# A layer with two FFNs and a mixer: the order of the next FFN's row sums against a norm's root

## The chip, the cores and the metric

The kernel runs on one core of a Trainium2 chip. The core has a matrix engine (TensorE, PE in the profile), a vector engine (VectorE, DVE), a scalar engine (ScalarE, ACT), GpSimd (POOL) and SyncE (SP), which here issues the transfers between device memory and the core's memories. Each engine works off its own list of instructions in a fixed order, and waits by semaphores for what other engines deliver. The metric is the device time of one execution in microseconds, the median over some runs.

## The reference

One layer on a sequence of 1024 tokens with width 1024, in three parts, each added to the stream `x`: a first FFN (SwiGLU, inner width 2816), a mixer, and a second FFN. Each part starts with a norm that is modulated by numbers from a condition vector:

```
mod = silu(cond) @ w_mod + b_mod;  sh1, sc1, g1, ..., sh3, sc3, g3 = split(mod, 9)
h  = modulate(rms_norm(x, mix_norm), sh2, sc2);  b, c, v, u = split(h @ w_in)
yA = b * conv3(c * v);  yB = GLU(ssm(u))
x  = x + g2 * ([rms_norm(yA) | rms_norm(yB)] @ w_out)
h  = modulate(rms_norm(x, ffn2_norm), sh3, sc3)
x  = x + 0.5 * g3 * (silu(h @ w_gate) * (h @ w_up)) @ w_down
```

Shift, scale and gate (`sh3`, `sc3`, `g3`) of the second FFN depend on the condition alone. They are 3 x 1024 dot products of length 1024.

## The kernel before

Activations lie with the width on the 128 partitions and tokens along the free axis, in two halves `h` of 512 tokens; a width of 1024 makes 8 tiles `d` or `k`. Every operand of a product is split into a high part (rounded to fp32r) and a low part, and a product is three matrix products (`mm3`, from line 337). Weights stream through two raw buffers (loaded on SP), and `Weights.pump` splits each: ACT casts the high part, DVE subtracts to get the low part. Split weights go to a ring of four tiles in this stage; a tile comes free when its last product is done.

In the mixer, PE does in this order: products for `u`, `c`, `v` with the state-space work between, the `b` products, the GLU products (`gl`, in `glu`), and the output products (`wo`, in `w_out`). Two norms are needed ahead of `wo`: that of the conv part (`nA`, halves `nAa`, `nAb`) and that of the SSM part (`nBa`, `nBb`). A norm goes like this: squares on ACT, added up on DVE; PE sums over partitions (tile `...st`); `roots` runs nine small DVE instructions on 128 x 4 numbers; `wide` widens the result to 128 x 512 (`...rb`), and adds that instruction to the list `widened`; PE spreads it over the partitions (`...bc`, in `spread`); DVE scales (`oat`, `obt`) and ACT and DVE split (`oa`, `ob`). The norm of the second FFN follows in the same way, as `n3a` and `n3b`; there some of the sums of squares are added on POOL.

The dot products for the second FFN's modulation are made on DVE beside all this. `mod_fetch` loads a tile of 128 x 1024 of transposed `w_mod` into one of two buffers `wm`; `mod_vector` multiplies it by the broadcast condition and sums each row into one column of `scl`, `mods` or `gate`. There are 24 of these reductions (in the profile `wm<-wm,cact`, each with a read of the accumulator): 8 for the scale, then 8 for the shift, then 8 for the gate. Each is followed by the fetch for the one two places later.

When each of them is emitted is set by a `Clock` that ticks with every `mm3`. Work that is due after so many ticks is emitted then (`clock.after`), and every `clock.period` ticks one step of a side generator is taken; `side2` gives one reduction per step. In the mixer the period is 8 during the second half of the `b` products, 1000 (none) during `glu` and the first `w_out` calls, and 3 from the call `w_out((2, 3), 1, 0)` on; what is left is emitted behind `w_out((4, 5, 6, 7), 0, 1)`.

The order of emission is not that of execution. From this point of the program on (`InOrder.strict` is false) the framework's planner fixes each engine's order before the run: in a simulated time of its own cost model, an engine takes the first instruction in program order among those whose inputs and buffers it believes ready. An instruction emitted late can so be placed early on its engine, into a gap that the planner sees. `InOrder.follow` adds an edge without a semaphore between two instructions of one engine: the first argument may not be placed ahead of the second.

Of the kernel before, what the change touches and what calls it, by code (L numbers as in the profile page):

```python
# [17 lines left out]
ALU = mybir.AluOpType  # L18
# [217 lines left out]
def hymba_layer(ctx: ExitStack, tc, x_d, xt_d, wm1_d, wmod_d, gu1_d, gs1_d, ds1_d, wl1_d, win_d, wout_d, glu_d, gu2_d, gs2_d, wd2_d, ds2_d, wl2_d, cols_d, cond_d, lam_d, bc_d, out_d):  # L236
    nc = tc.nc
    V, A, T, SP = (InOrder(tc, e) for e in (nc.vector, nc.scalar, nc.tensor, nc.sync))
# [15 lines left out]
    pools = {}  # L254
# [158 lines left out]
    widened = []  # L413
# [52 lines left out]

    def mod_vector(w, s):

        V.tensor_tensor_reduce(out=w, in0=w, in1=pools["cact"][:], scale=1.0, scalar=0.0, op0=ALU.mult, op1=ALU.add, accum_out=s)

    later = [(n, b, i) for n in (G1, SC2, SH2, G2, SC3, SH3, G3) for b in range(4) for i in range(2)]
    fetched = deque()
# [8 lines left out]
    def mod_tile(home):  # L481

        n, d, r = fetched.popleft()
        dst = (mods, scl, gate)[n % 3][:, n // 3]
        mod_vector(r, dst[:, d : d + 1])
        if d == KT - 1:
            mod_done(n, 0, KT, dst)
        mod_fetch(home)
# [308 lines left out]
    cact = pools["cact"] = cap.tile([P, 1024], F32, name="cact")  # L797
# [815 lines left out]
        gate_b(i, 0)  # L1613
    clock.until(lambda: NB - 1 not in held)
    sp_open.close()
    yp2 = es2.enter_context(tc.tile_pool(name="yp2", bufs=1))
    yb = [yp2.tile([P, S], F32, tag=f"yb{i}", name=f"yb{i}") for i in range(4)]
    mods_open = ExitStack()
# [74 lines left out]
        clock.step()  # L1693
    clock.period = 4
    mods_open.close()
    es2.close()
    movs["B"] = ctx.enter_context(tc.tile_pool(name="movB", bufs=12))
    norm_into(act3, 0, n3[0], 2, "h3", "B", copied3)
# [180 lines left out]
```

## Time and profile before

| what | us |
|---|---|
| median of 3 runs | 1709.91 |
| runs | 1709.65, 1709.91, 1714.65 |
| profiled execution, its time | 1713.61 |
| span in its trace, first to last instruction | 1711.8 |
| PE busy | 1668.0 (97%) |
| DVE busy | 1250.9 (73%) |
| ACT busy | 624.3 (36%) |
| POOL busy | 402.7 (24%) |

A row of a timeline gives the start from the beginning of the span, the length (of all that are merged in it), the engine, the line of the kernel, the operation, the tiles written and read, the shapes and the number of instructions; in brackets stands how long the engine was idle before it, and what ended that. Line 112 is the helper through which every call goes, so groups are told apart by the tiles' names. A row of stretches gives for each engine its busy time and, in brackets, its instructions, then the granted clock of PE, the share of the transfers and their rate.

### The profile page before, as it was taken

To read this page: it belongs to the slowest core of one execution; us is meant where nothing else is said; L and a number is where in the kernel's file an instruction comes from. 1 tells how busy PE (TensorE), PEld (TensorE's weight loads), DVE (VectorE), ACT (ScalarE), POOL (GpSimd) and SP (SyncE) were. 2 spreads that over 40 slices of the span, in tenths; PEclk is the share of its full clock that TensorE was granted. 3 is DMA by queue.
4 is the path that set the end of the run, shared out by engine and by line. 5 is a ranking of instruction groups with operands and counts; after the bars stand their busy time and mean duration, and the time that the engine had idled before them with its cause. 6 is when DMAs were issued, how large, how long until landed. Compare 5 with 4: busy or idle time off the path is not lost.

```text
span 1711.8 us, 20820 instructions
## 1 busy us (share of the span) xinstructions
PE 1668.0 (97%) x7532; PEld 1369.1 (80%) x7532; DVE 1250.9 (73%) x1957; ACT 624.3 (36%) x1056; POOL 402.7 (24%) x309
## 2 busy tenths in 40 slices
PE   7999999999999999999999999999999999999997
PEld 4888787888878778787877778888888888888886
DVE  7739698899588997635657877957777767576645
ACT  5425333333354332332214325524444434322233
POOL 6012333323222322100000021122233223333212
PEclk8999999999999999999999999999999999999998
DMA  8312464454565656134644352324443343759212
GB/s 340 131 47 97 142 220 163 148 161 159 205 221 171 230 196 233 50 100 145 221 145 153 130 184 103 119 74 172 185 185 148 148 172 148 267 227 382 107 50 99
DMA packets 101625, 281.48 MB, mean 164 GB/s; under 512 B 19345, under 2 KB 34961, under 8 KB 90386
## 3 DMA queue, kind: packets, MB, share of 16 engines
q1 hardware_dynamic: 101522, 280.15, 46.5%
q8 instruction: 59, 0.97, 0.2%
q14 instruction: 44, 0.36, 0.1%
HBM read 195.69 MB, written 76.02 MB: 159 GB/s over the span
## 4 chain that ended last, share of the span: by engine, by line
PE 50%; DVE 4%; DMA 3%; issue 0%; ACT 0%; SPq 0%; DVEq 0%; ACTq 0%
PE wo L112 4%; PE fb10d L112 2%; PE u L112 2%; PE fbd_1B L112 2%; PE fbd_0B L112 2%; DMA swz<-si 2%; PE b L112 2%; PE c L112 1%; PE fb0u L112 1%; PE fbd_1C L112 1%; PE fbd_0C L112 1%; PE fbd_1A L112 1%; PE fbd_0A L112 1%; PE fb0d L112 1%; PE fb0g L112 1%; PE v L112 1%
## 5 line engine op out<-in xcount | busy, mean ns | idle before, releaser
L112 ACT CAST w<-raw 128x512 fp32r<-128x512 f32 (+1 forms) x374 | 240.3, 677 | 483.7 <-issue 77.1
L112 DVE TENSOR_TENSOR w<-raw,w 128x512 fp32r<-128x512 f32 (+1 forms) x374 | 307.0, 840 | 117.9 <-ACT w L112 117.0
L177 POOL TENSOR_TENSOR raw<-sums,raw 128x512 f32<-128x512 f32 x54 | 81.9, 1517 | 441.8 <-DVE w L112 429.5
L168 POOL TENSOR_TENSOR sums<-raw 128x512 f32<-128x512 f32 x54 | 75.4, 1396 | 266.7 <-DMA raw<-in_ds 136.4
L179 POOL TENSOR_TENSOR raw<-raw 128x512 f32<-128x512 f32 x54 | 83.3, 1543 | 82.0 <-DVE w L112 82.0
L112 DVE CUSTOM_DVE_ANT_0 wm<-wm,cact 128x1024 f32<-128x1024 f32 x56 | 78.0, 1406 | 11.0 <-DMA wm<-in_wmod 10.7
L169 POOL TENSOR_TENSOR raw<-raw 128x512 f32<-128x512 f32 x54 | 84.5, 1565 | 4.2
L370 POOL TENSOR_TENSOR n3aq<-n3aq,n3aq 128x512 f32<-128x512 f32 x5 | 7.7, 1532 | 275.5 <-ACT n3aq L112 275.3
L112 DVE TENSOR_TENSOR w<-sums,w 128x512 fp32r<-128x512 f32 x54 | 54.1, 1013 | 2.7 <-ACT w L112 2.2
L112 PE MATMUL p<-h,w 128*128 128x512 f32 x192 | 51.5, 420 | 1.7 <-ACT h L112 1.7
L112 PE MATMUL wo<-oa,w 128*128 128x512 f32 x192 | 46.1, 393 | 1.2 <-DVE w L112 0.7
L112 PE MATMUL v<-h,w 128*128 128x512 f32 x192 | 46.9, 395 | 0.0
L112 PE MATMUL c<-h,w 128*128 128x512 f32 x192 | 46.6, 394 | 0.0
L112 PE MATMUL b<-h,w 128*128 128x512 f32 x192 | 45.6, 393 | 0.0
L112 PE MATMUL wo<-ob,w 128*128 128x512 f32 x192 | 45.5, 392 | 0.1
L112 PEld LDWEIGHTS p<-h,w 128*128 128x128 f32 x192 | 37.1, 200 | 10.1 <-ACT h L112 1.9
L112 PE MATMUL u<-h,w 128*128 128x512 f32 x192 | 44.8, 392 | 0.2 <-DVE h L112 0.2
L112 ACT CAST w<-sums 128x512 fp32r<-128x512 f32 x54 | 32.8, 620 | 31.8 <-PE fa4gE L112 2.2
L112 PEld LDWEIGHTS wo<-oa,w 128*128 128x128 f32 x192 | 35.7, 188 | 9.7 <-DVE w L112 1.1
L112 PEld LDWEIGHTS u<-h,w 128*128 128x128 f32 x192 | 35.7, 188 | 8.3 <-DVE h L112 0.6
L112 PEld LDWEIGHTS wo<-ob,w 128*128 128x128 f32 x192 | 35.7, 188 | 7.8 <-ACT ob L112 0.5
L112 PEld LDWEIGHTS b<-h,w 128*128 128x128 f32 x192 | 35.5, 188 | 7.2
(1579 smaller groups left out, 4054.0 us busy)
## 6 DMA issues: line engine op xcount, KB each, us to landing
raw<-in_gs SPq DMA_DIRECT2D x38, 1024.0 KB, 4.9
wm<-in_wmod SPq DMA_DIRECT2D x56, 512.0 KB, 4.8
raw<-in_ds SPq DMA_DIRECT2D x16, 1024.0 KB, 6.6
mw<-in_wm SPq DMA_DIRECT2D x8, 1024.0 KB, 7.6
raw<-in_win SPq DMA_DIRECT2D x8, 1024.0 KB, 5.9
raw<-in_gu SPq DMA_DIRECT2D x6, 1024.0 KB, 5.3
raw<-in_wl SPq DMA_DIRECT2D x5, 1024.0 KB, 6.7
xb<-in_xt SPq DMA_DIRECT2D x8, 512.0 KB, 6.8
```

Source lines behind the costliest of these rows:

```text
L112: r = getattr(self.engine, name)(*args, **kw)
L168: self.G.tensor_tensor(out=f, in0=r[2], in1=r[1], op=ALU.subtract)
L169: self.G.tensor_tensor(out=r[1], in0=r[1], in1=r[0], op=ALU.subtract)
L177: self.G.tensor_tensor(out=r, in0=s["t3"], in1=r, op=ALU.add)
L179: self.G.tensor_tensor(out=r, in0=self.chunk(j, 3), in1=r, op=ALU.subtract)
L370: nc.gpsimd.tensor_tensor(out=a, in0=a, in1=sq[:, :n], op=ALU.add)
```

## The change

While the mixer runs (a mark `mixed` in `pools`, set where the SSM buffers are closed and taken away when the mixer's buffers are), every reduction of `mod_vector` gets an edge to the last element of `widened`, that is, to the last root that had been widened by then in program order. The planner may not place the reduction ahead of it on DVE.

```
     def mod_vector(w, s):
 
-        V.tensor_tensor_reduce(out=w, in0=w, in1=pools["cact"][:], scale=1.0, scalar=0.0, op0=ALU.mult, op1=ALU.add, accum_out=s)
+        r = V.tensor_tensor_reduce(out=w, in0=w, in1=pools["cact"][:], scale=1.0, scalar=0.0, op0=ALU.mult, op1=ALU.add, accum_out=s)
+        if "mixed" in pools:
+            V.follow(r, widened[-1])
...
     sp_open.close()
+    pools["mixed"] = True
...
     mods_open.close()
+    pools.pop("mixed")
     es2.close()
```

## The prediction

> **What bounds the kernel now.** The reductions are numbered R1 to R24 in program order: R1 to R8 make `scl`, R9 to R16 `mods`, R17 to R24 `gate` of the second FFN. I read the page first, for the engine with the work.
>
> ```profile
> PE 1668.0 (97%) x7532; PEld 1369.1 (80%) x7532; DVE 1250.9 (73%) x1957; ACT 624.3 (36%) x1056; POOL 402.7 (24%) x309
> ```
>
> PE is busy for 97%, so only time in which PE stands still, or runs at a lower clock, can be gained. Next, what PE waited for (us in total, times, longest); the rows of the mixer behind its gate products are these:
>
> ```profile
> PE nBabc L112 <- DVE nBarb L112: 2.3, 1, 2.3
> PE nAbbc L112 <- DVE nAbrb L112: 1.7, 1, 1.7
> PE gl L112 <- DVE yg L112: 1.7, 1, 1.7
> PE nBbbc L112 <- DVE nBbrb L112: 0.7, 1, 0.7
> PE wo L112 <- DVE w L112: 0.7, 1, 0.7
> ```
>
> Two of them, the first and the last but one, wait for a widened root of the SSM norm (`nBa`, `nBb`). The timeline of DVE shows what stood in front of these roots (start, length):
>
> ```profile
> 948.39 0.16 DVE L112 TENSOR_SCALAR nBanv<-nBast 128x4 f32<-128x4 f32 x1 [0.25 <-PE nBast L112]
> 949.06 0.16 DVE L112 TENSOR_SCALAR nBani<-nBanv 128x4 int32<-128x4 int32 x1
> 949.13 1.22 DVE L112 CUSTOM_DVE_ANT_0 wm<-wm,cact 128x1024 f32<-128x1024 f32 x1
> ...
> 951.44 1.23 DVE L112 TENSOR_TENSOR w<-raw,w 128x1024 fp32r<-128x1024 f32 x1 [1.01 <-ACT w L112]
> 952.58 0.15 DVE L112 TENSOR_TENSOR nBana<-nBana,nBanv 128x4 f32<-128x4 f32 x1
> 952.65 1.22 DVE L112 CUSTOM_DVE_ANT_0 wm<-wm,cact 128x1024 f32<-128x1024 f32 x1
> 953.80 0.16 DVE L112 SCALAR_TENSOR_TENSOR nBany<-nBana,nBani 128x4 f32<-128x4 f32 x1
> ...
> 954.78 0.43 DVE L112 TENSOR_SCALAR nBarb<-nBany 128x512 f32<-128x512 f32 x1
> 955.12 1.22 DVE L112 CUSTOM_DVE_ANT_0 wm<-wm,cact 128x1024 f32<-128x1024 f32 x1
> ...
> 970.19 1.22 DVE L112 CUSTOM_DVE_ANT_0 wm<-wm,cact 128x1024 f32<-128x1024 f32 x1
> 973.79 1.22 DVE L112 CUSTOM_DVE_ANT_0 wm<-wm,cact 128x1024 f32<-128x1024 f32 x1
> 977.00 0.43 DVE L112 TENSOR_SCALAR nBbrb<-nBbny 128x512 f32<-128x512 f32 x1
> ```
>
> These `wm` rows are reductions: R5 and R6 (949.13, 952.65) sit inside the chain of small root instructions of `nBa`, R7 and R8 behind it (R7 is shown), R9 and R10 (970.19, 973.79) ahead of the widened root of `nBb`. Between them `w`, the low part of a weight tile, waits 1.01 us for ACT. PE and its clock just behind (two rows of its timeline, the chain's row for twelve `gl` products and one for full speed, and between them two stretches, whose third figure from the end is the granted clock):
>
> ```profile
> 955.35 1.36 PE L112 MATMUL nBabc<-ident,nBarb 128*128 128x128 f32 x8 [2.30 <-DVE nBarb L112]
> 937.29 1.16 PE L112 MATMUL nAbbc<-ident,nAbrb 128*128 128x128 f32 x8 [1.75 <-DVE nAbrb L112]
> 956.71 4.13 PE gl L112 x12
> 956.00:958.00 2.00, 2.00 (x9) 1.71 (x8) 1.94 (x5) 1.01 (x2) 0.00 (x0) 0.53 0.56 162
> 958.00:960.00 2.00, 2.00 (x7) 1.52 (x7) 2.00 (x4) 0.22 (x1) 0.00 (x0) 0.62 0.77 233
> 1049.62 5.44 PE fb0g L112 x24
> ```
>
> After the wait the granted clock falls to 0.53 and 0.62. The twelve `gl` products take 4.13 us; 24 products at full clock take 5.44, so twelve take 2.72. The fall costs about 1.4 us on `gl` and, by the 1.36 of `nBabc` against the 1.16 us of the same eight products of `nAbbc`, 0.2 more: **1.6 us**.
>
> **The change part by part.** Counted along the program's ticks: R1 is emitted before any root of the mixer, R2 to R4 after `nAa` was widened, and R5 to R24 from the first tick of the second `w_out` pair on, after `nBb`. So R1 to R4 keep their place (the 1.7 us waits at `gl` and `nAbbc` stay), and R5 to R10 can't start until `nBbrb` has been issued. No instruction is added or removed; six of 1.22 us, their accumulator reads, and the DMA issues on SP that refill their two buffers, are moved.
>
> *The nBa wait.* Without R5 and R6 the chain is `nBani` at 949.06, then seven steps at 0.2 us each (from 953.80 to 954.78 there are five, in 0.98 us), and `nBarb` with 0.43: it starts near 950.6 and is done near 951.1. PE finishes its `gl` products at 953.05 (955.35 less 2.30). The low part of the weights is the doubt. If it stays behind the first step, it still ends near 952.58, for it waits for ACT, and only R6 goes: the step that started at 953.80 starts 0.2 us after 952.58, 1.02 us sooner, and so does `nBarb`. If it comes behind the root, the whole 2.30 goes. The planner took it only after 1.2 us of R5, and the chain to the root lasts 1.5 us, so it lands near its end; each step behind it then costs 0.2. I take **1.8 us**, between 1.02 and 2.30.
>
> *The clock.* A wait of 0.5 us in place of 2.30 should not lower it: the wait of 1.7 us at `gl` left it at 1.00, as a stretch of 10 us shows (same columns),
>
> ```profile
> 920.00:930.00 10.00, 7.98 (x39) 6.11 (x38) 7.14 (x18) 5.21 (x9) 0.00 (x0) 1.00 0.00 2
> ```
>
> so 1.6 us would go, from the profiled execution. The Trainium skill, "TensorE: Matmul & The Clock Gate", Part 1, has the clock halve after an idle window of about 3.4 us that runs freely, at another phase in every run; by its length alone the wait of 2.30 us would not do it, and the trace has it fall. By its free phase a fall need not come in each execution; then the 1.6 us is not in all of them.
>
> *The nBb wait.* R9 and R10 leave that chain, 2.4 us of work; `nBbrb`, now at 977.00, is then ready before PE comes, even when updates of `x` stay among its steps. The whole **0.7 us**; nothing at the least, if a weight tile takes their place.
>
> *What is late next.* The reductions end in the same DVE queue, later. Behind `nBbrb` both buffers are full, so R5 and R6 run at once; the others are paced by their transfers:
>
> ```profile
> 978.91 1.23 DVE L112 CUSTOM_DVE_ANT_0 wm<-wm,cact 128x1024 f32<-128x1024 f32 x1 [1.49 <-DMA wm<-in_wmod]
> 990.64 1.72 POOL L370 TENSOR_TENSOR n3bq<-n3bq,n3bq 128x512 f32<-128x512 f32 x1 [14.49 <-ACT n3bq L112]
> 991.13 2.31 DVE L112 CUSTOM_DVE_ANT_0 wm<-wm,cact 128x1024 f32<-128x1024 f32 x1
> 1014.15 1.23 DVE L112 CUSTOM_DVE_ANT_0 wm<-wm,cact 128x1024 f32<-128x1024 f32 x1 [3.47 <-DMA wm<-in_wmod]
> 1024.21 1.23 DVE L112 CUSTOM_DVE_ANT_0 wm<-wm,cact 128x1024 f32<-128x1024 f32 x1 [1.21 <-DMA wm<-in_wmod]
> 1025.36 2.72 DVE L112 SCALAR_TENSOR_TENSOR x<-wo,gate,x 128x512 f32<-128x512 f32 x4
> 1034.03 0.43 DVE L112 TENSOR_SCALAR n3arb<-n3any 128x512 f32<-128x512 f32 x1
> 1014.95 11.04 PE L112 MATMUL wo<-ob,w 128*128 128x512 f32 x48
> 1031.27 0.95 PE L112 MATMUL n3ast<-one,n3aq 128*128 128x1 f32 x8
> 1036.99 1.05 PE L112 MATMUL n3abc<-ident,n3arb 128*128 128x128 f32 x8
> 1097.72 21.76 PE fb0d L112 x96
> ```
>
> From R20 (1014.15) to R24 (1024.21) a reduction takes 2.5 us. At 978.91 R11 ran in the profile; after the change that place is R7's, so the tail lags by four, 10 us at most: R24 at 1034 in place of 1024. Its results are not the limit: `gate` is read behind the first down products, on PE from 1097.72, and with a lag of four R16, the last for `mods`, runs where R20 does now, at 1014.15, while its reader needs `n3abc` at 1036.99. SP issues the refills in one queue with the raw weights; a refill now waits until after `nBbrb`, and a raw load put behind it by the planner would wait too. No row of PE's waits in the mixer names a transfer, so I put that at nothing, with a delay of the last weights (0.7 us of wait now) as the risk. What is exposed is what stands **behind a reduction on DVE**: the four updates of `x`, the squares and their sums, PE's `n3ast`. In the profile R24 already holds up the first update: its products, nine before the end of the 48, are done at 1025.99 - 9 x 0.227 = 1023.95, and it starts at 1025.36. `n3ast` then follows with no idle time on PE. So whatever PE gains before, it meets a chain that was just in time. If the reductions keep their place before `x` and their clock time, the gain stops there and all of it is given back; if `x` goes first, 1.4 us of cover is free, and each reduction put between `x` and `n3arb` takes 1.22 us and, at the pace of the transfers, up to 2.5. The root itself ends at 1034.46 and has 1036.99 - 1034.46 = 2.5 us to spare. The planner knows both, so it puts `x` first when it believes it ready; I take **0.9 us** given back, with 0 and the full 2.5 as bounds of this case. A reduction beside POOL's adds takes longer (2.31 us at 991.13, with an add on POOL from 990.64 for 1.72). The Trainium skill, "SBUF — State Buffer", on the shared port pair, explains such a row by an exclusive lock between DVE with two SBUF inputs and POOL; by it each of the moved reductions that meets an add would cost DVE 1.1 us more, which the bounds above already hold.
>
> *The sum.* 1.8 + 0.7 - 0.9 = 1.6 us without the clock, 3.2 with it. The profiled execution took 1713.61 us, so it would take 1710.4. It is one of the slower ones: the median of the runs is 1709.91, 3.7 below, which is more than the fall of the clock at 956 costs, so I do not count on that fall in the median. 1709.91 - 1.6 = **1708.3 us**; between 1706.7 with the clock and 1709.9 with nothing kept, which is this case's own range.
>
> **Rivals.** *(1) All is handed back at `n3ast`.* For it: PE's arrival there has no cover, and the transfers of `wm` run by the clock, not by PE. Against it: R24 can now go behind `x`. Time: 1709.9, to 1711 with a wait left over.
>
> *(2) The full gain.* The low part goes behind the root, the clock no longer falls in the timed runs either, nothing is given back: 2.3 + 1.6 + 0.7 = 4.6, so 1705.3. For it: the fall is there in the one profile. Against it: the slack of `n3ast`.
>
> *(3) Slower: reductions inside the `n3a` chain.* The same thing that holds up `nBa` now happens 80 us later, where the planner finds R20 to R24 outstanding and fills the gaps between `x`, the sums and the root of `n3a`. The chain from the first `x` (1025.36) to `n3ast` lasts 5.9 us. With four of them there at 2.5 us, 10 us are added; 1.4 of cover and the gain of 2.5 come off, some 6 remain: 1716. It decides from the point where more than two reductions, 5 us, are inside. Against it: DVE stands idle for 3.47 and 1.21 us ahead of R20 and R24, so the queue can catch up before it comes to `x`.
>
> *(4) The order binds nothing* is excluded for R5 to R10, which run before `nBbrb` now.
>
> **How the numbers follow.** Chances: forecast 0.42, (1) 0.25, (2) 0.18, (3) 0.15. The range from 1704.5 to 1713.5 leaves out the upper half of (3) and the best of (2). A measurement of this kernel tells about 0.3%, 5.1 us, from no change. Faster by more, below 1704.8, needs (2) with something on top, say the 0.7 us at the weights of the last `w_out` and a second fall of the clock: 0.1. Slower by more is most of (3): 0.1. The rest, 0.8, is within.
>
> **What would show it.** Right: no `wm` reduction between `nBanv` and `nBbrb`; `nBabc` with a wait under 1.3 us; `nBbbc` with none; a clock of 1.00 from 956 to 960. R24 ends after 1025 and `x` of the last four comes before it. Wrong: a new wait of PE at `n3ast` or `n3abc`, with a `wm` row just in front on DVE, or a new one at `wo` behind its weights. If PE's waits in the mixer are gone and the time is still that of before, the loss lies behind 1050, and my reading that nothing there depends on DVE's order is wrong.

## The result, and the profile after

Both kernels ran eleven times on one chip. The changed kernel took **1717.7 us** (median), the kernel before 1712.88; the ratio is 1.0026, with an interval of 1.0015 to 1.0038: slower by 4.5 us, between 2.6 and 6.5. The prediction was 1708.3 us, a gain of 1.6. Its sign is wrong, and the time lies above its range. A part of the distance is the level: two of the three runs of before that were shown, 1709.65 and 1709.91, are at the low end of the 81 runs of that kernel in the comparisons of this document (1707.45 to 1720.83). The rest, a loss of 4.5 us by these runs and of about 3 by the stretches below, in place of a gain of 1.6, is the change.

The profiled execution took 1716.45 us, with a span of 1714.7. First PE's waits in the mixer (us in total, times, longest). The waits at `nBabc` and `nBbbc` are gone; there is a new one at `n3ast`, and a longer one at the weights of the last `w_out`, for ACT:

```profile
PE n3ast L112 <- DVE n3aq L112: 3.0, 1, 3.0
PE wo L112 <- ACT w L112: 1.3, 1, 1.3
```

DVE's timeline at the root of `nBa` answers to the one shown of before:

```profile
950.00 0.16 DVE L112 TENSOR_SCALAR nBanv<-nBast 128x4 f32<-128x4 f32 x1 [0.26 <-PE nBast L112]
...
952.05 0.16 DVE L112 SCALAR_TENSOR_TENSOR nBany<-nBana,nBany 128x4 f32<-128x4 f32 x1
953.05 1.23 DVE L112 TENSOR_TENSOR w<-raw,w 128x1024 fp32r<-128x1024 f32 x1 [0.84 <-ACT w L112]
954.19 0.42 DVE L112 TENSOR_SCALAR nBarb<-nBany 128x512 f32<-128x512 f32 x1
```

No reduction stands in it. The low part `w` still comes ahead of `nBarb`, which is done at 954.61, 4.6 us after the chain began, in place of 6.8 (948.39 to 955.21). PE's timeline from there on:

```profile
939.81 5.73 PE L112 MATMUL wo<-oa,w 128*128 128x512 f32 x24
...
954.76 1.13 PE L112 MATMUL nBabc<-ident,nBarb 128*128 128x128 f32 x8
955.64 3.01 PE L112 MATMUL gl<-yg,w 128*128 128x512 f32 x12
...
972.37 1.05 PE L112 MATMUL nBbbc<-ident,nBbrb 128*128 128x128 f32 x8
...
1001.97 1.65 PE L112 MATMUL wo<-oa,w 128*128 128x512 f32 x6 [1.34 <-ACT w L112]
...
1011.95 11.04 PE L112 MATMUL wo<-ob,w 128*128 128x512 f32 x48
...
1031.90 1.87 PE L112 MATMUL n3ast<-one,n3aq 128*128 128x1 f32 x8 [3.02 <-DVE n3aq L112]
1033.63 6.82 PE L112 MATMUL wo<-ob,w 128*128 128x512 f32 x19
1040.29 1.05 PE L112 MATMUL n3abc<-ident,n3arb 128*128 128x128 f32 x8
...
1063.90 1.05 PE L112 MATMUL n3bbc<-ident,n3brb 128*128 128x128 f32 x8
```

The mixer delivers: PE reaches the 48 products at 1011.95, against 1014.95 before, although this execution was 1.6 us behind when it began with `wo` (939.81; before it was 938.20). Then all of it is lost at `n3ast`, and more: PE stands still for 3.02 us, the eight one-column products take 1.87 us in place of 0.95, and nineteen products behind them 6.82, where 21 took 5.07. The stretches there (PE's busy time first, third from the end its granted clock):

```profile
1030.00:1032.00 2.00, 0.10 (x1) 0.10 (x1) 1.84 (x4) 0.00 (x0) 0.00 (x0) 0.90 0.68 209
1032.00:1034.00 2.00, 2.00 (x9) 2.00 (x10) 0.16 (x1) 0.00 (x0) 0.00 (x0) 0.50 0.17 61
1034.00:1036.00 2.00, 2.00 (x6) 1.52 (x6) 1.90 (x8) 0.00 (x0) 0.00 (x0) 0.50 0.00 0
1036.00:1038.00 2.00, 2.00 (x6) 1.56 (x5) 0.97 (x6) 0.00 (x0) 0.00 (x0) 0.50 0.00 0
1038.00:1040.00 2.00, 2.00 (x9) 1.62 (x8) 0.00 (x0) 0.00 (x0) 0.00 (x0) 0.89 0.00 0
```

The missing clock of the five stretches, 0.20 + 3.00 + 0.22 us, makes 6.8 us at half speed; by finer stretches it begins at 1031.6, 0.3 us before the wait ends. What PE waited for stands in DVE's timeline:

```profile
1021.86 1.23 DVE L112 CUSTOM_DVE_ANT_0 wm<-wm,cact 128x1024 f32<-128x1024 f32 x1 [2.04 <-DMA wm<-in_wmod]
...
1023.01 0.75 DVE L112 SCALAR_TENSOR_TENSOR x<-wo,gate,x 128x512 f32<-128x512 f32 x1
1024.30 1.23 DVE L112 CUSTOM_DVE_ANT_0 wm<-wm,cact 128x1024 f32<-128x1024 f32 x1 [0.54 <-DMA wm<-in_wmod]
...
1025.45 2.07 DVE L112 SCALAR_TENSOR_TENSOR x<-wo,gate,x 128x512 f32<-128x512 f32 x3
1027.43 2.01 DVE L112 CUSTOM_DVE_ANT_0 wm<-wm,cact 128x1024 f32<-128x1024 f32 x1
...
1029.37 0.68 DVE L112 TENSOR_TENSOR n3aq<-n3aq,n3aq 128x512 f32<-128x512 f32 x1
1030.01 1.23 DVE L112 CUSTOM_DVE_ANT_0 wm<-wm,cact 128x1024 f32<-128x1024 f32 x1
...
1031.16 0.68 DVE L112 TENSOR_TENSOR n3aq<-n3aq,n3aq 128x512 f32<-128x512 f32 x1
...
1034.68 1.22 DVE L112 CUSTOM_DVE_ANT_0 wm<-wm,cact 128x1024 f32<-128x1024 f32 x1
...
1036.61 0.43 DVE L112 TENSOR_SCALAR n3arb<-n3any 128x512 f32<-128x512 f32 x1
```

R20 runs where R24 ran. R21, R22 and R23 stand between the first update of `x` and the last sum of squares, and R24 in the root. From the first `x` to the end of the last sum it is 1031.84 - 1023.01 = 8.8 us. The three cost 0.54 + 1.15 + 1.94 + 1.15 = 4.8 us (the first term is the wait for R21's transfer, the others go from start to start; R22 runs beside an add on POOL, 1.29 us from 1027.07). Of the kernel before, these rows of the same place were not shown yet, with the two of PE that are used further down:

```profile
938.20 5.73 PE L112 MATMUL wo<-oa,w 128*128 128x512 f32 x24
...
1029.61 0.69 DVE L112 TENSOR_TENSOR n3aq<-n3aq,n3aq 128x512 f32<-128x512 f32 x1 [1.38 <-POOL n3aq L370]
1030.41 0.69 DVE L112 TENSOR_TENSOR n3aq<-n3aq,n3aq 128x512 f32<-128x512 f32 x1
...
1032.08 5.07 PE L112 MATMUL wo<-ob,w 128*128 128x512 f32 x21
...
1060.61 1.05 PE L112 MATMUL n3bbc<-ident,n3brb 128*128 128x128 f32 x8
```

There it is 5.7 us, from 1025.36 to 1031.10, and DVE stood idle for 1.38 of them; into that gap a part of the 4.8 us falls, and the chain is 3.1 us longer. R24 costs nothing here: `n3arb` is done 3.2 us before PE, slowed by its clock, comes to `n3abc`.

From here on I cut each execution at four rows of PE: the first 24 `wo` products behind `nAbbc`, the second group of 48 `wo` products, `n3abc` and `n3bbc`. In the changed kernel these are 939.81, 1011.95, 1040.29 and 1063.90, and the end of the span. The kernel before was profiled three more times (below).

| us | A: `wo` to the 48 | B: to `n3abc` | C: to `n3bbc` | A+B+C | D: to the end |
|---|---|---|---|---|---|
| before, four profiles | 76.75, 74.76, 76.34, 74.79 | 22.04, 22.37, 21.98, 23.03 | 23.62 each | mean 121.64 | 650.6 to 651.7 |
| changed, two profiles | 72.14, 72.21 | 28.34, 28.67 | 23.61, 23.62 | mean 124.30 | 650.8, 651.1 |

By their means, A is shorter by 75.66 - 72.18 = 3.5 us and B longer by 28.50 - 22.36 = 6.1; C is the same, and in D no difference shows beside its spread of 1.1 us. The net is 2.7 us slower, within the interval of the timed runs. This also leaves out the scatter of what lies ahead: the first row, which stands ahead of the first reduction that the change moves, came anywhere from 935.5 to 942.0 us in the fourteen profiles of this study. A part of that scatter is a fall of the clock behind the 1.7 us wait at `gl`: it is in eight of the fourteen, in both of the changed kernel and in one of the four of the kernel before. Whether the change has a part in that is not shown; A, B and C do not hold it.

### The profile page after: what moved, and what is told of

Its sections match the earlier page's. It is cut to its first block, busy times and chain, and to the rows that moved or that the text cites. A ratio compares the mean times of both kernels' runs of the same rounds, so it can differ in the third digit from the quotient of the medians.

```text
span 1714.7 us, 20822 instructions
## 1 busy us (share of the span) xinstructions
PE 1671.4 (97%) x7532; PEld 1371.8 (80%) x7532; DVE 1250.2 (73%) x1957; ACT 624.9 (36%) x1056; POOL 405.9 (24%) x309
## 4 chain that ended last, share of the span: by engine, by line
PE 50%; DVE 4%; DMA 3%; issue 1%; SPq 0%; ACT 0%; DVEq 0%; ACTq 0%
PE wo L112 3%; PE fb10d L112 2%; PE u L112 2%; PE fbd_1B L112 2%; PE fbd_0B L112 2%; PE v L112 2%; PE b L112 2%; DMA swz<-si 1%; PE c L112 1%; PE fb0u L112 1%; DMA wm<-in_wmod 1%; PE fbd_1C L112 1%; PE fbd_0C L112 1%; PE fbd_1A L112 1%; PE fbd_0A L112 1%; PE fb0d L112 1%
```

## The experiments

The theory after the result was the prediction's third rival: reductions late in the queue stand in the `n3a` chain, and this makes both the wait and the fall of the clock behind it. Against it stood: the clock falls there for another reason; something is lost behind the mixer; transfers are late. The timed comparisons are against the kernel before, run on the same chip in the same session, its median 1713.87 in the first four and 1713.66 in the next four (35 runs each, 12 of each experiment).

**The last four reductions left out** (from the changed kernel and from the one before):

```
-    later = [(n, b, i) for n in (G1, SC2, SH2, G2, SC3, SH3, G3) for b in range(4) for i in range(2)]
+    later = [(n, b, i) for n in (G1, SC2, SH2, G2, SC3, SH3, G3) for b in range(4) for i in range(2)][:-4]
...
+    V.memset(gate[:, 2, 4:], 0.0)
+    mod_done(G3, 0, KT, gate[:, 2])
```

> The changed kernel without the last four reductions (R21 to R24): their transfers and sums are left out, and the four columns of the gate are set to zero. Theory (the loss sits in the chain from the last updates of x to n3ast, where three of the four stand, and in the root, where the fourth stands): PE's wait of 3.0 us at n3ast and the fall of the clock behind it go, 5 to 7 us less than the changed kernel, so 3 to 4 us under the kernel before. Rival (the loss is elsewhere, the mixer's gain is not worth what the trace shows): within 1.5 us of the changed kernel, that is 3 to 5 us above the kernel before.

> The kernel before without the same four reductions (left out in the same way). Theory: n3ast has no wait in the kernel before, so within 1 us of it. Rival (fewer reductions are worth time wherever they are): as much less than the kernel before as the changed kernel gains from leaving them out, 5 to 7 us.

Their transfers go too, and half of the second FFN's gate is zero, so these two kernels do less than the layer asks. From the changed kernel: 1711.03 us, ratio 0.9979 (0.9964 to 0.9994), faster than before. From the kernel before: 1714.31, ratio 0.9998 (0.9985 to 1.0011). So the same four reductions cost nothing that can be measured where they ran before, and some 5 us where they run now (A, B and C together 119.06 us against 124.30). PE at `n3ast` in the changed kernel without them:

```profile
1029.93 1.05 PE L112 MATMUL n3ast<-one,n3aq 128*128 128x1 f32 x8 [0.81 <-DVE n3aq L112]
1030.84 5.04 PE L112 MATMUL wo<-ob,w 128*128 128x512 f32 x21
1035.72 1.05 PE L112 MATMUL n3abc<-ident,n3arb 128*128 128x128 f32 x8
```

The clock is full, B is 23.09 us, and 0.81 us of wait is left. That is the most that PE's earlier arrival alone can cost here, close to the 0.9 of the prediction; but one of the four profiles of the kernel before has 0.77 us of wait and a B of 23.03 as well. A stays at 72.35. In the kernel before without them, `nBabc` waited its 2.30 us as ever, but the twelve products behind it took 3.00 us:

```profile
953.99 1.13 PE L112 MATMUL nBabc<-ident,nBarb 128*128 128x128 f32 x8 [2.30 <-DVE nBarb L112]
954.88 3.00 PE L112 MATMUL gl<-yg,w 128*128 128x512 f32 x12
```

The fall of the clock that I had priced at 1.6 us is not in this execution; more profiles of the kernel before follow below.

**The last four, or the last two, held back until the root of `n3a` is widened.** The side generator stops at the 20th (22nd) reduction; the rest are emitted behind that root (the clock's period is 1000 until then), and the buffer that shares their memory is opened after them:

```
+            while done == pools.get("most"):
+                yield
...
+    pools["most"] = 20
...
-    while clock.side:
-        clock.step()
...
+        if ds[0] == 4:
+            pools.pop("most")
+            pools["mixed"] = True
+            while clock.side:
+                clock.step()
```

> The changed kernel with all its work, but R21 to R24 emitted behind the widened root of n3a and ordered after it. Theory: no reduction in the n3a chain, so the wait at n3ast and the fall of the clock go as in the kernel without them, 3 to 4 us under the kernel before; if the four now hold up the modulated rows (2.5 us of slack there), up to 3 us of this comes back as a wait of PE at the first products of the FFN. Rival: within 1.5 us of the changed kernel.

> The changed kernel with R23 and R24 alone emitted and ordered behind the root of n3a; R21 and R22 stand among the last updates of x. Theory: two of the three reductions ahead of n3ast and the one in the root are gone or moved, the wait at n3ast is 1 to 2 us in place of 3.0, and the two that are held run while DVE waits for PE, so the FFN's first products don't wait as with four (1.4 us there): 2 to 4 us under the changed kernel. Rival (what was gained by holding four came from something else than their places): the same as the changed kernel.

With four held: 1713.92 us, ratio 0.9999 (0.9985 to 1.0013). `n3ast` waits 0.47 us at full clock and B is 22.77, but C is 26.52 in place of 23.62. DVE and PE of this kernel:

```profile
1039.86 1.73 DVE L112 CUSTOM_DVE_ANT_0 wm<-wm,cact 128x1024 f32<-128x1024 f32 x1
...
1042.02 1.23 DVE L112 CUSTOM_DVE_ANT_0 wm<-wm,cact 128x1024 f32<-128x1024 f32 x1 [0.43 <-DMA wm<-in_wmod]
...
1043.99 0.69 DVE L112 TENSOR_TENSOR h<-h3t,h 128x512 fp32r<-128x512 f32 x1
```

```profile
1054.87 1.67 PE L112 MATMUL fb0g<-h,w 128*128 128x512 f32 x6 [0.65 <-DVE h L112]
1056.72 0.74 PE L112 MATMUL fb0g<-h,w 128*128 128x512 f32 x2 [0.18 <-DVE h L112]
...
1058.51 0.96 PE L112 MATMUL fb0u<-h,w 128*128 128x512 f32 x3 [0.58 <-DVE w L112]
```

The last two now stand ahead of the modulated rows `h` of the second FFN, whose first products wait. A, B and C together are 121.94 us: with no reduction in the `n3a` chain most of its loss is gone, and about half of that comes back here. With only the last two held: 1716.23 us, ratio 1.0009 (0.9995 to 1.0023), and nothing is won at `n3ast`. DVE of this kernel:

```profile
1025.84 0.75 DVE L112 SCALAR_TENSOR_TENSOR x<-wo,gate,x 128x512 f32<-128x512 f32 x1
1027.59 2.18 DVE L112 CUSTOM_DVE_ANT_0 wm<-wm,cact 128x1024 f32<-128x1024 f32 x1 [1.00 <-DMA wm<-in_wmod]
...
1029.69 2.06 DVE L112 SCALAR_TENSOR_TENSOR x<-wo,gate,x 128x512 f32<-128x512 f32 x3
1031.67 1.98 DVE L112 CUSTOM_DVE_ANT_0 wm<-wm,cact 128x1024 f32<-128x1024 f32 x1
...
1033.59 1.48 DVE L112 TENSOR_TENSOR n3aq<-n3aq,n3aq 128x512 f32<-128x512 f32 x2
```

Two reductions in the chain, R21 and R22, cost as much as three in the changed kernel: 1.00 of waiting for a transfer with three updates of `x` behind it, then 2.10 and 1.92, both while POOL adds squares (1.29 us from 1027.39, 1.27 from 1031.31). PE waits 3.85 us at `n3ast` and B is 28.69. So my point from which the third rival decides, more than two inside, was wrong.

**Thirteen more products on PE ahead of `n3ast`**, into a tile of which only the part is read that the sums overwrite; they fill the wait:

```
+                if self.name == "n3a":
+                    whole_st = sm([P, HALF], self.name + "st")
+                    st = whole_st[:, :4]
+                    for _ in range(13):
+                        T.matmul(whole_st[:], lhsT=wsel(wo[7], 0)[0], rhs=actA[1][0][0], start=True, stop=True)
```

> The changed kernel with 13 more products of 128x512 on PE (their result is overwritten) just ahead of n3ast: they take 2.95 us at full clock and fill the wait. Nothing else moves. Theory (half of the loss is the clock that falls behind the wait: n3ast 1.87 us in place of 0.95 and 19 products in 6.82 us in place of 4.3): the clock stays at 1.00 and the time is 2.5 to 3.3 us under the changed kernel. Rival (the fall of the clock costs nothing that counts, the wait is all): the same as the changed kernel within 1 us.

1715.25 us, ratio 1.0014 (0.9997 to 1.0032): the interval holds no change as well as what the changed kernel loses, so the timed runs don't decide. In the profile 0.90 us of the wait are left, and the clock falls all the same, but for half as long (0.55 and 0.60 in two stretches of 2 us from 1032 on). B is 27.72. The filler took 3.11 us for 2.1 us of wait, and one of two falls went: 1.0 lost, 1.7 won, which is the difference in B. So in this one execution the low clock is a cost of its own behind the wait.

**The edge for all of them to the root of `nBa` at the latest**, so that R7 and later may run sooner than in the changed kernel:

```
-            V.follow(r, widened[-1])
+            V.follow(r, widened[min(len(widened), 5) - 1])
```

> The changed kernel with the edges tied to the root of nBa at the latest, not to that of nBb: R5 and R6 leave the chain of nBa, R7 and R8 stand in that of nBb, the tail lags by two in place of four. Theory (what counts is how many reductions stand between the last updates of x and n3ast; here it is still three, R22 to R24, and none in the root): the wait for nBa goes, the 0.7 us for nBb stays, n3ast waits between 1 and 3 us, and the time is 0 to 3 us over the kernel before. Rival (the loss goes with the lag: two in place of four): half the loss, 1 to 2 us under the changed kernel, from the reductions' own time and not from their places.

1717.21 us, ratio 1.0016 (1.0000 to 1.0032). The queue is less late, yet R22, R23 and R24 (1023.18, 1027.23, 1029.75) still stand ahead of the last sum, R22 with 1.03 us of waiting for its transfer; `n3ast` waits 4.20 us, more than I had expected, and B is 28.05. One thing came out that had not been asked: `nBbbc` waits 0.89 us again, and A is 72.11, no longer than the 72.14 of the changed kernel. In this kernel the wait for ACT at the last `w_out` is gone. What the changed kernel wins at `nBb` it pays back there, 30 us later, and the cause is a reduction once more. These are rows of DVE and ACT in the changed kernel:

```profile
997.50 2.09 DVE L112 CUSTOM_DVE_ANT_0 wm<-wm,cact 128x1024 f32<-128x1024 f32 x1 [1.50 <-DMA wm<-in_wmod]
...
999.52 1.40 DVE L112 SCALAR_TENSOR_TENSOR x<-wo,gate,x 128x512 f32<-128x512 f32 x2
1000.36 0.63 ACT L112 ACTIVATE n3bq<-x 128x512 f32<-128x512 f32 x1 [1.35 <-DVE x L112]
1000.89 1.03 ACT L112 CAST w<-raw 128x1024 fp32r<-128x1024 f32 x1
```

The cast for which PE waits until 1001.97 stands on ACT behind a square of `x`, and that update of `x` stands on DVE behind a reduction. In the kernel with the edge to `nBa` no reduction delays this `x` (it starts at 998.02, as soon as PE delivers it), and the cast is done at 1000.55.

**R5 and R6 behind the root of `nBa`, all later ones as in the change, the last three held back** as above (`most` is 21):

```
-            V.follow(r, widened[-1])
+            made.append(r)
+            V.follow(r, widened[4 if len(made) in (5, 6) else -1])
```

> A version meant to keep the gain: R5 and R6 ordered behind the root of nBa, R7 on behind that of nBb, R22 to R24 held behind the root of n3a. Theory: both waits in the mixer go (3.0 us), no reduction stands between the last updates of x and n3a's root, one stands in front of the modulated rows (up to 1 us): 1.5 to 3 us under the kernel before. Rival (PE's arrival at n3ast has no cover, so any gain ends there): a wait of 2 to 3 us at n3ast without any reduction in the chain, and the time of the kernel before.

1712.66 us, ratio 0.9991 (0.9979 to 1.0003). A is 71.80 and B 22.03, with no wait at `n3ast`: R21, the last ahead of the chain, is done at 1019.5, before PE has the products for the first `x`. C is 25.01, 1.4 more than before, for R24 stands ahead of the rows `h` again and 0.59 us of wait appear at the first `fb0u`. A, B and C together are 2.8 us under the mean of before. It is the best version with all its work, but the timed runs don't tell it from the kernel before.

**The changed kernel again**, beside these three:

> The changed kernel once more, beside the kernel before on the same chip. It should come out 3 us over it: PE gains the 3.0 us of its waits for the roots of nBa and nBb in every execution (the clock's fall behind nBa is not in every one), and gives back 3.0 us of wait at n3ast and 3.1 us of half clock behind it. If the first comparison was off by chance, it lies within 1 us of it.

1716.39 us, ratio 1.0010 (0.9997 to 1.0023). By itself this could still be no change (-0.5 to 3.9 us); the interval of the first comparison (2.6 to 6.5) overlaps with it from 2.6 to 3.9, and the stretches above have 2.7. The wait at `n3ast` was 3.58 us, and the clock was at half for as long as the first time.

**The kernel before, profiled three more times**, and once **with ten products ahead of `nBabc`**, whose result is overwritten:

> The kernel before, unchanged, looked at again. Open is whether the clock falls behind `nBabc`'s wait in every execution. If the fall belongs to the wait: `nBabc` again waits 2.3 us and the 12 `gl` products behind it take about 4.5 us, and from the first `wo` x24 behind `nAbbc` to `n3bbc` it is 122.4 us. If the fall comes and goes (it was absent once in the kernel before without its last four reductions): the 12 products take 3.0 us and the stretch is about 120.8 us.

> As before_2: 122.4 us for the stretch and about 4.5 us for the 12 `gl` products if the fall belongs to the 2.3 us wait; 120.8 us and 3.0 us if it comes and goes.

> As before_2: 122.4 us and 4.5 us if the fall belongs to the wait; 120.8 us and 3.0 us if it comes and goes.

```
+        if nm == "nBa":
+            for _ in range(10):
+                T.matmul(bc[:], lhsT=wsel(wgl[0], 0)[0], rhs=actG[0][0][0], start=True, stop=True)
```

> The kernel before, with ten products of 128x512 issued ahead of `nBabc` (about 2.4 us of tensor-engine work in place of its 2.3 us wait; their result is overwritten). If the fall follows the wait: `nBabc` waits under 0.3 us, the clock stays at 1.00 from 950 to 965, the 12 products take 3.0 us and the stretch from the first `wo` x24 to `n3bbc` is about 120.9 us. If the fall comes from something else at that place: the products take up to 4.5 us all the same and the stretch is about 122.5 us.

`nBabc` waited 2.30 us in each of the three; the twelve products behind it took 3.02, 4.59 and 3.02 us. With the profile of before and the kernel without its last four reductions, the fall was there in two executions of five, after the same wait. It is worth 1.8 us when it comes, which is the difference between the means of A (76.75 and 76.34 against 74.76, 74.79 and 74.71), and 0.7 on average. With the ten products `nBabc` had no wait and the clock stayed full, but A was 75.19, not shorter: the products cost what the wait had cost, 0.83 us of wait at `nBbbc` stayed, and PE waited 1.35 for ACT at the last `w_out`. Its one time, 1710.26 us beside 1714.66, says nothing of the edit: its first row of A came at 935.46, 2.7 us sooner than in any profile of the kernel before, ahead of the place of the edit. In one of the three profiles (A 74.79) PE waited 0.77 us at `n3ast`, so in the kernel before, too, PE comes there just about in time.

## Why the prediction was wrong

- **The nBa wait** (1.8, between 1.02 and 2.30): right in mechanism, and the whole 2.30 went. The low part of the weights did stay ahead of `nBarb`, as I had feared, but DVE took no R5 in front of the root instructions, so that they were all done by 952.2 and `nBarb` came right behind `w`. The 1.8 was 0.5 too small because I let steps of the root wait behind `w`; none did.
- **The nBb wait** (0.7): gone as predicted, but worth about nothing. PE came sooner to the last `w_out` and waited there 1.34 us for ACT's cast in place of 0.51. The prediction had put a delay of the last weights at nothing and named it as the risk, by way of their transfers; it was not a transfer of weights, but a reduction in front of the `x` that ACT needed first (the rows are shown above).
- **The clock** (1.6, not counted): leaving it out of the median was nearly right, it comes in two executions of five. My reason that a wait of 1.7 us at `gl` leaves the clock alone came from one profile; in eight of the fourteen it fell there. And I only asked whether the old fall goes, not where the next one would be. The new wait of 3.0 us has its own, and twice as long.
- **The lag of four**: right, in part by luck. R20 is 7.7 us late (1021.86 in place of 1014.15), less than the 10 of the forecast; R24 runs at 1034.68, close to the 1034, because it was placed into the root behind the delayed `n3ast`.
- **"I take 0.9 us given back, with 0 and the full 2.5 as bounds"**: this step failed. `x` does go first, but only its first update; then the planner put R21, R22 and R23 between the others and the sums. B became 6.1 us longer. The wait at `n3ast` is 3.0 to 3.6 us of it, and the clock behind it about 3 (missing between the end of the wait and the end of the fall: 3.3 and 3.0). Where no reduction is in the chain, PE waited 0.81, 0.47 and 0 us: the 0.9 was at most the price of PE's arrival alone, and its bound of 2.5 had room for two reductions at the least time and for one at the pace of the transfers, though the text named 1.22 to 2.5 us for each; the low clock behind a wait was not in it at all.
- **Rival (3)** describes what happened, with a chance of 0.15 in place of the 0.42 of the forecast. My reason against it, that DVE stands idle for 3.47 and 1.21 us ahead of R20 and R24 and so could catch up, was the error: these gaps are waits for the transfer of the next tile. DVE waits 2.04 us at 1021.86 after the change, too; by then the queue has caught up 2.4 of the four places' 10 us (R20 at 1021.86, where R24 ran at 1024.21), for its transfers set its pace and not DVE's idle time. Its sum had other parts than the real one: 10 us for four reductions, of which 6 stay, against 3.1 us more in the chain and a clock that it did not hold. It expected 6 us more than before; about 3 were measured.
- **Rival (1)**, all handed back at `n3ast`, is not what happens: without reductions in the chain the gain of A stays, but for 0.7 us at most (B of 23.09 against 22.36), and the time with them left out is 2.8 us better.
- **D**, behind `n3bbc`: 650.6 to 652.0 us in all fourteen profiles. Nothing behind the stretches is seen to depend on this order, as the prediction said.

In sum: 2.3 at `nBa`, 0.9 of the clock (in two of the four profiles of before) and 0.3 of smaller gaps are won, 3.5 together; 6.1 are lost at `n3ast`.

## What to carry to other kernels

Work that ran at the pace of its transfers was hardly made up here once it was late: whoever delays its head delays its tail, and should first look at which chain lies at the new end and how much slack that has. Hold the tail back as well as the head, or the planner puts it into the next chain of small dependent steps, which has the same gaps as the first. A wait of PE of 2.3 to 3.6 us cost up to twice its length here, so compare waits by whether the clock falls behind them, over more than one execution.

## What the runs showed of the hardware

The clock falls in portions. Over 920 to 1062 us, the sum of the missing clock over stretches of 2 us, (1 - clock) x 2 us, was at each place where it fell either 1.70 to 1.72 us or 3.40 to 3.42, in each of the eleven profiles with a fall: half speed for 3.4 us, or for 6.8. The stretches of the kernel with the edge to `nBa` are a single portion, although its wait was the longest of all, 4.20 us, and `n3ast` itself still ran at full speed:

```profile
1032.00:1034.00 2.00, 2.00 (x11) 1.71 (x11) 1.07 (x7) 0.00 (x0) 0.00 (x0) 0.66 0.04 8
1034.00:1036.00 2.00, 2.00 (x6) 1.52 (x5) 0.83 (x4) 0.00 (x0) 0.00 (x0) 0.50 0.00 0
1036.00:1038.00 2.00, 2.00 (x10) 1.66 (x9) 0.00 (x0) 0.00 (x0) 0.00 (x0) 0.98 0.00 0
```

The missing clock of these is 0.68 + 1.00 + 0.04 = 1.72 us; the five of the changed kernel, shown above, give 0.20 + 3.00 + 0.22 = 3.42. The Trainium skill, "TensorE: Matmul & The Clock Gate", Part 1, has a window of 3.4 us that runs freely, with full or half speed and nothing between; the portions agree with that. So do the places of the falls: by stretches of a quarter of a us they last 3.41 or 6.83 us, and in each of the four profiles with a fall both at `gl` and at `n3ast` the two begin 105.8 us apart, 31 times 3.413. That it takes a whole idle window, as the page has it, these runs do not bear out: the wait of `nBabc` is 2.30 us, and in the kernel with thirteen more products it was 0.90.

At `n3ast` the clock fell in all five profiles with a wait made by reductions (0.90 us with the products, 3.02, 3.58, 3.85, 4.20), and in none of the nine others, among them waits of 0.47, 0.77, 0.81 and 0.97 us. One count fits what decides. A fall fixes the grid of its execution, so the eleven profiles can be cut into windows of 3.413 us, from 890 to 1060 us. For each window I add the time in which PE stood still and that of its one-column products (tiles `...st`). Behind a window at full clock with 1.95 us or more, the next one was at half speed, eleven times of eleven; with 1.74 or less, never; between them both occurred, four times and six. Without the one-column products no such limit shows: there was a fall behind 0.77 us of standing still, and none behind 1.84. The wait of 2.30 us at `nBabc` lay whole in one window or with 1.95 us of it, and the clock fell; in a third profile an edge of the grid left 1.84, and it didn't. The wait of 0.90 us shared its window with 1.05 us of `n3ast`, 1.95 together, and that of 0.81 with 0.85, 1.66 together. This is worked out from the runs afterwards; no run was made to test it, and where no fall fixes the grid, as in the profile with 0.97 us, it says nothing.
